# Two-level Strassen products in an MLP kernel: product 6 is also done in seven quarter products, and a pair's steps stand in another order

## The chip, the cores and the metric

The kernel runs on one core of one Trainium2 chip. The metric is device time in microseconds (us): the median of several executions of the whole kernel. The engines are named as in the profile: PE is the matmul engine (TensorE), PEld its weight loads, DVE is VectorE, ACT is ScalarE, POOL is GpSimd, SP is SyncE, which here issues transfers.

## The reference, cut to what matters

```python
batch, seq_len, hidden_dim = 8, 1024, 1024
intermediate_dim = 4 * hidden_dim

h = x @ w1                                   # [8192,1024] @ [1024,4096]
h = 0.5 * h * (1 + np.tanh(np.sqrt(2 / np.pi) * (h + 0.044715 * h ** 3)))
return (h @ w2).astype(np.float32)           # [8192,4096] @ [4096,1024]
```

Two large matrix products with a GELU between them. All of `x`, `w1`, `w2` arrive as float32 in device memory; the matmuls run on float16 copies and accumulate in float32.

## The kernel before, in words

**Blocks of tokens.** The 8192 tokens are worked in eight blocks of 1024 (`sb` 0 to 7). For each block a first stage computes `g = gelu(x @ w1)` and a second stage `g @ w2`. For blocks 0 and 1 the stages are `matmul1` and `matmul2_made`, which also build the operand sums and store them in device memory. For blocks 2 to 7, the late blocks, they are `matmul1_late` and `matmul2`, which load the stored sums. The change is about `matmul1_late`.

**Strassen, twice.** Every big product is cut in 2 by 2 blocks and done by the Winograd form of Strassen's method: seven products (numbered 1 to 7) of sums of blocks in place of eight. The dictionaries `W_SUM` and `S_SUM` name the sums: 5, 6, 7 and 4 on one side, 7, 6, 5 and 3 on the other. In the late blocks some of the seven products are cut once more in the same manner, into seven quarter products of half the size each way. In `matmul1_late` these are products 1, 5, 2 and 3; products 6, 7 and 4 are done whole. One whole product of a pair is two halves of four matmuls with 512 columns. One product of the second level is seven parts of two matmuls with 256 columns.

**Pairs.** `matmul1_late` goes through the 4096 intermediate columns in eight pairs (`Pair`, j = 0 to 7) of two chunks of 128 columns in each half of the intermediate dimension. A pair uses eight PSUM banks: a, b, c and d, each twice (h = 0, 1). In bank a, product 1 is followed by 6, 7 and 4; bank c holds 5, b holds 2, d holds 3.

**The order of the work is written out by hand.** The list `PAIR` is a string of keys, and `Pair.run` turns one key into instructions. `m` and `i` is a quarter product (`m15` is part 5 of product 1); `h60` is half 0 of the whole product 6; `c`, `a`, `p` and the keys `z11`, `z51` are ACT copies out of PSUM; the other `z`, the `e`, `s` and `u` are DVE additions; `g` is a GELU on ACT into the tile `g`; `d` is the subtraction `difference`. A key with a prime belongs to the previous pair, so that the end of one pair is woven into the next. After the last pair the list is walked once more for its primed keys alone: this is the tail of the stage. Every one of these instructions keeps its program order on its engine.

**What a product of the second level needs beside the matmuls.** For products 2 and 3 the base is a temporary (`a` or `s`); two DVE additions `e` add part 5 into it, and four DVE additions `z` write base plus running sum into the four quarters of the two banks, each between two parts. For products 1 and 5, whose base is zero, two of these steps are ACT copies.

**Operand sums.** The inner sums of the weights come from device memory (`s2`, `s3`; `s1` and `s5` for pairs 1 and 2) or are made on POOL from pair 3 on (`StoredHalf.make`, four operations a pair, one pair ahead). `StoredHalf` loads the weights of one pair in six groups (`GROUPS`) by SP's queue, two pairs ahead, into tiles of the pool `up` (26 tiles of 512 KB). The inner sums of x are made on DVE in tiles of the pool `gcp` (4 tiles): for product 2 in the stage before, for 1, 3 and 5 at the places that `X_SUMS` names, in pairs 0 and 1. Pair 0 does products 1 and 5 whole (`whole`), since the sums are not ready.

**Other work of the stage.** POOL also casts x of the next block through device memory (`x_cast_paced`, pairs 0 to 3; each starts behind a tiny copy that waits for a tile), does `difference`, and makes one sum for the second stage (`early.make(7, ...)`, after pair 5, into a `gcp` tile). In block 1, `matmul1` carries the `split_in_m1` jobs: the four inner sums of the second weight matrix for products 2 and 3, with loads and stores of their own.

## Time and profile before

| | us |
|---|---|
| median of 3 executions (1466.79 to 1467.35) | 1466.9 |
| the profiled execution's own time | 1466.68 |
| its span, first to last instruction | 1464.9 |
| PE busy in the span | 1456.8 (99%) |
| DVE busy | 1166.0 (80%) |
| ACT busy | 600.7 (41%) |
| POOL busy | 443.6 (30%) |
| one first stage of a late block (404.18 to 492.76) | 88.58 |
| one second stage of a late block (492.76 to 580.51) | 87.75 |

The page's own warning matters here: matmuls are pipelined and their ends are modelled, so a busy PE says nothing of how far apart the matmuls start. Durations are those of single instructions; where instructions follow each other closely, the distance between their starts is shorter than the duration, and it is the distance that counts in a queue. The granted clock of PE was 1.000 over the span.

### The profile page before, as it was taken

What the parts mean: (1) busy time and instruction counts of PE and PEld (TensorE: products, weight loads), DVE (VectorE), ACT (ScalarE), POOL (GpSimd) and SP (SyncE); (2) the same over time, 40 slices, a digit from 0 to 9 for tenths busy, and PEclk for the clock granted to TensorE, in tenths of its full rate; (3) what the DMA queues carried; (4) which work ended last, traced back from release to release, by engine and by line L of the source; (5) the groups of instructions that cost most, each with busy time, mean ns of one, the idle gap of its engine ahead of it and who ended that gap; (6) DMA issues with size and microseconds to landing.
All of it is one profiled execution on the core that took longest, in us unless ns stands there. A gap on an engine that the chain in (4) does not pass through costs nothing.

```text
span 1464.9 us, 27508 instructions
## 1 busy us (share of the span) xinstructions
PE 1456.8 (99%) x10383; PEld 1012.9 (69%) x10383; DVE 1166.0 (80%) x1940; ACT 600.7 (41%) x1226; POOL 443.6 (30%) x471
## 2 busy tenths in 40 slices
PE   8999999999999999999999999999999999999998
PEld 5444444444466788668876688767887678866787
DVE  6657459757677899879997799977998779887897
ACT  5665125631066411663126621366214652056410
POOL 1441123312347011560026501274103721136011
PEclk9999999999999999999999999999999999999999
DMA  9999899998998999979999899998999999996896
GB/s 330 342 349 392 229 342 360 385 300 230 353 323 215 360 276 366 375 207 373 307 369 338 203 373 326 359 305 248 350 346 347 297 280 313 352 367 215 310 302 206
DMA packets 207429, 462.15 MB, mean 315 GB/s; under 512 B 75840, under 2 KB 80960, under 8 KB 206400
## 3 DMA queue, kind: packets, MB, share of 16 engines
q1 hardware_dynamic: 179808, 364.96, 72.4%
q0 software_dynamic: 27488, 95.44, 21.9%
q8 instruction: 81, 1.33, 0.3%
q14 instruction: 52, 0.43, 0.1%
HBM read 361.76 MB, written 113.25 MB: 324 GB/s over the span
## 4 chain that ended last, share of the span: by engine, by line
PE 99%; DMA 1%; SPq 0%; DVE 0%; issue 0%; DVEq 0%
PE ps L1018 35%; PE ps L485 31%; PE ps L699 19%; PE ps L1059 13%; PE ps L418 1%; DMA gc<-in_w_dram 1%; SPq L159 0%; PE ps L395 0%; DVE u L223 0%; DVE u L135 0%; DVE u L406 0%; DVEq L135 0%
## 5 line engine op out<-in xcount | busy, mean ns | idle before, releaser
L485 PE MATMUL ps<-u 128*128 128x512 f16 x1808 | 423.5, 379 | 0.0
L135 DVE TENSOR_TENSOR tmp<-tmp,ps 128x512 f32<-128x512 f32 x498 | 280.3, 581 | 106.0 <-PE ps L485 44.6
L162 ACT COPY tmp<-ps 128x512 f32<-128x512 f32 (+1 forms) x398 | 209.4, 545 | 259.4 <-PE ps L1059 135.2
L135 DVE TENSOR_TENSOR ps<-tmp,ps 128x256 f32<-128x256 f32 x552 | 222.7, 425 | 102.9 <-PE ps L699 83.7
L1018 PE MATMUL ps<-u,gc 128*128 128x256 f16 x2688 | 300.3, 273 | 0.0
L485 PEld LDWEIGHTS <-u 128*128 128x128 f16 x1808 | 176.9, 98 | 170.2
L1018 PEld LDWEIGHTS <-gc 128*128 128x128 f16 x2688 | 263.0, 98 | 30.4
L699 PEld LDWEIGHTS <-u 128*128 128x128 f16 x2170 | 212.3, 98 | 67.9 <-issue 0.4
L498 ACT ACTIVATE g<-ps 128x512 f16<-128x512 f32 x326 | 192.9, 596 | 105.3 <-PE ps L699 64.9
L135 DVE TENSOR_TENSOR u<-u 128x2048 f16<-128x2048 f16 (+3 forms) x288 | 214.7, 787 | 23.6 <-DMA w_d<-u 10.9
L1018 PE MATMUL ps<-u,g 128*128 128x256 f16 x2016 | 227.9, 273 | 0.0
L162 ACT COPY u<-ps 128x512 f32<-128x512 f32 (+1 forms) x134 | 78.0, 587 | 354.9 <-PE ps L1018 348.0
L805 POOL DMA_DIRECT2D out_dram<-u x70 | 63.9, 936 | 498.2 <-DVE u L135 264.9
L1018 PEld LDWEIGHTS <-g 128*128 128x128 f16 x2016 | 197.2, 98 | 22.8
L699 PE MATMUL ps<-u 128*128 128x256 f16 x1298 | 193.6, 273 | 0.0
L135 DVE TENSOR_TENSOR u<-u,ps 128x512 f32<-128x512 f32 x216 | 147.7, 684 | 36.5 <-PE ps L1018 25.3
L1059 PE MATMUL ps<-u,g 128*128 128x512 f16 x768 | 166.4, 379 | 0.0
L498 ACT ACTIVATE g<-tmp 128x512 f16<-128x512 f32 x186 | 117.4, 633 | 99.0 <-DVE tmp L135 98.7
L306 POOL TENSOR_TENSOR u<-u 128x512 f16<-128x512 f16 x120 | 136.3, 1157 | 31.8 <-PE ps L699 22.4
L699 PE MATMUL ps<-gc,u 128*128 128x256 f16 x872 | 145.7, 273 | 0.0
L1059 PEld LDWEIGHTS <-g 128*128 128x128 f16 x768 | 75.1, 98 | 90.6
L1012 DVE TENSOR_TENSOR gc<-g,gc 128x2048 f16<-128x2048 f16 x84 | 102.4, 1220 | 3.1 <-PE ps L1018 3.1
(52 smaller groups left out, 854.8 us busy)
## 6 DMA issues: line engine op xcount, KB each, us to landing
u<-w_d SPq DMA_DIRECT2D x322, 512.0 KB, 9.1
u<-in_d SPq DMA_DIRECT2D x168, 512.0 KB, 7.9
out_dram<-u POOLq DMA_DIRECT2D x70, 512.0 KB, 10.8
gc<-in_w_dram SPq DMA_DIRECT2D x48, 512.0 KB, 6.0
g<-w_d SPq DMA_DIRECT2D x40, 512.0 KB, 12.0
w_d<-u POOLq DMA_DIRECT2D x36, 512.0 KB, 7.5
w_d<-u SPq DMA_DIRECT2D x32, 512.0 KB, 9.2
xb<-in_x_dram POOLq DMA_DIRECT2D x56, 256.0 KB, 6.8
```

The source lines that it names most:

```text
L135: i = nc.vector.tensor_tensor(out=out, in0=in0, in1=in1, op=op)
L162: tc.keep_in_program_order(nc.scalar.copy(out=out, in_=in_))
L306: nc.gpsimd.tensor_tensor(out=operand(j), in0=operand(u), in1=operand(v), op=op)
L418: tc.keep_in_program_order(nc.tensor.matmul(bank[:, cols], lhsT=w[:, k, :], rhs=self.xs.blocks[f"{a}{r}"][:, k, cols], start=r == 1 and k ...
L485: tc.keep_in_program_order(nc.tensor.matmul(bank, lhsT=w, rhs=x, start=first and k == 0, stop=k == n - 1, skip_group_check=not first,))
L498: gelu_last[0] = nc.scalar.activation(out=out, in_=src, func=GELU)
L699: tc.keep_in_program_order(nc.tensor.matmul(out, lhsT=w, rhs=x, start=first and k == 0, stop=k == 1, skip_group_check=not first,))
L805: return nc.gpsimd.dma_start(out=rows, in_=src, **kw)
L1012: tc.keep_in_program_order(engine.tensor_tensor(out=self.s[j], in0=in0, in1=in1, op=op))
L1018: tc.keep_in_program_order(nc.tensor.matmul(bank[:, i * OH // 2:(i + 1) * OH // 2], lhsT=t[:, c, i * P:(i + 1) * P], rhs=self.y[j][:, c, : ...
L1059: tc.keep_in_program_order(nc.tensor.matmul(pair(bank), lhsT=a[:, c, :], rhs=chunks(pieces[c // QC])[:, :, c % QC, :], start=(first and c ...
```

## The change

Product 6 joins the products of the second level in `matmul1_late`, from pair 1 on; pair 0 does 1, 5 and 6 whole. Its seven parts go into bank a, in which product 1 lay. The base of its additions is the ACT copy of product 1 (`temp a`), which was made before too, for product 2. Its first part starts the accumulation in bank a, h = 1, afresh. Two new DVE additions (`f60`, `f61`) write base plus part 5 into a new temporary `q`, because the copy itself is changed later by the additions `e` of product 2; four DVE additions `z61` to `z64` write the quarters. Added for this are the weight sums `s6`, which share a group with product 6 while 7 now shares one with 4, their making and storing in blocks 0 and 1 (`inner_sums(6)`), and four inner sums of x for product 6, in a fourth `gcp` tile. The sum that `early.make(7, ...)` makes goes to a tile of `up` instead.

The list `PAIR` is a new order. Products 2, 3, 6 (second half), 7 and 4 of a pair now run mostly within the next pair's walk. Pair 0 has a list of its own, `PAIR_FIRST`, and the sums of x stand there (four) and in pair 1 (the others). `difference` of pair 0 moves from DVE to POOL, and the first x cast of a stage waits for a sum of x instead of a GELU. `split_in_m1` is gone: its sums for products 2 and 3 are made in `matmul2_made` of block 0, as `split_jobs`, like that of product 1, in units of `up`.

```diff
-GROUPS = ((1, 5), ("s1", "s5"), (2, "s2"), (6, 7), (3, "s3"), (4,))
+GROUPS = ((1, 5), ("s1", "s5"), (2, "s2"), (6, "s6"), (3, "s3"), (7, 4))
...
+m15 m11 m51 e20' m26' z62' z53' z11 m55 m67' m63' c1 m54' p1' z22' z63' m27' z64' m23' c5 s0' m12
+m16 z12 z23' m22' m31' g110' m64' z24' s1' m35' h70' z31' m24' g111' m17 h71' z51 e31' z13 m36'
+u0' m14 a1 e30' m32' m56 h40' z32' m37' g210' z52 m13 m65 u1' m61 m53 z33' a0 m52 z34' f61 z61 m21
+m33' m25 h41' m62 f60 p0 m66 g221' g120' m57 g211' d' g220' e21 m34' z21 g121'
 """.split()
...
+PAIR_FIRST = """
+m11 i35 m21 m14 a0 i55 m25 a1 m51 p0 i65 e21 m61 i15 z21
 """.split()
-SPLIT_IN_M1 = (2, 3)
+X_SUMS = {
+    "g211'": ("i67",),
+    "c1": ("i66",),
+    "m56": ("i54",),
+    "z51": ("i14",),
+    "g121'": ("i64",),
+    "s0'": ("i17",),
+    "e20'": ("i16",),
+    "m23'": ("i57",),
+    "m37'": ("i34",),
+    "m26'": ("i36",),
+    "m67'": ("i56",),
+    "z22'": ("i37",),
+}
...
-            inner = ((2, 5, 3) if second else (1,)) if q == 0 else ((2, 3) if second else ())
+            inner = (2, 3) if second else (6,)
+            if q == 0:
+                inner += (5,) if second else (1,)
...
-            self.whole = (1, 5) if j == 0 else ()
+            self.whole = (1, 5, 6) if j == 0 else ()
...
-            b = {1: "a", 5: "c", 2: "b", 3: "d"}[m]
-            first = h == 1 and (b, 1) not in self.banks
+            b = {1: "a", 5: "c", 2: "b", 3: "d", 6: "a"}[m]
+            first = h == 1 and m not in self.begun
...
+            elif kind == "f":
+                add(temp("q", 0)[:, right if i else left], bank("a", 1)[:, right], temp("a", i)[:, right])
             elif kind in "ez":
-                b, t = ("b", "a") if m == 2 else ("d", "s")
+                b, t = {2: ("b", "a"), 3: ("d", "s"), 6: ("a", "a")}[m]
...
-                    add(bank(b, h)[:, cols], z, temp(t, h)[:, cols])
+                    base = temp(t, h)[:, cols]
+                    if m == 6 and cols == right:
+                        base = temp("q", 0)[:, right if h else left]
+                    add(bank(b, h)[:, cols], z, base)
...
-                spare = 0 < self.j < NI // 2 - 1
+                spare = self.j < NI // 2 - 1
...
-                    nxt["xb"] = x_cast_paced(sb + 1, g["11"][:, 2 * j, :], 2 * j, nxt.get("xb"), True)
+                    after = g["11"][:, 2 * j - 1, :] if j else xs.inner[5][:, 0, 0, :]
+                    nxt["xb"] = x_cast_paced(sb + 1, after, 2 * j, nxt.get("xb"), True)
...
-                early.make(7, nc.gpsimd)
+                early.make(7, nc.gpsimd, up, "u")
...
-        splits = {m: split_jobs(m, lambda m=m: pieces(m)) for m in (1, *SUMS)}
+        splits = {m: split_jobs(m, lambda m=m: pieces(m)) for m in (*W_TERM, *SUMS)}
```

More of the change, by code (lines that the diff above doesn't have):

```diff
@@ L28 @@
 PAIR = """
-m11 m36' m15 g111' z32' m21 h40' z11 c1 g221' m51 m37' g210' m55 z33' m25 c5 m12 z34' m16 z51
-h41' z12 m56 g211' m17 z52 m32' m13 z13 m33' a0 d' m52 m57 m53 g120' z21 m14 h60 p0 z53 e20 a1
-m54 s0 m34' p1 m26 m31 e21 m35 g121' h61 z22 z31 e30 m27 m22 s1 m23 h70 z23 g110 e31 z24 h71 u0
-m24 g220 u1
+m15 m11 m51 e20' m26' z62' z53' z11 m55 m67' m63' c1 m54' p1' z22' z63' m27' z64' m23' c5 s0' m12
+m16 z12 z23' m22' m31' g110' m64' z24' s1' m35' h70' z31' m24' g111' m17 h71' z51 e31' z13 m36'
+u0' m14 a1 e30' m32' m56 h40' z32' m37' g210' z52 m13 m65 u1' m61 m53 z33' a0 m52 z34' f61 z61 m21
+m33' m25 h41' m62 f60 p0 m66 g221' g120' m57 g211' d' g220' e21 m34' z21 g121'
 """.split()
-X_SUMS = """
-0z11:35 0z13:15 0z21:55 0z53:36 0a1:56 0m22:37 1m51:57 1m55:16 1m25:17 1z12:54 1m56:14 1h60:34
+PAIR_FIRST = """
+m11 i35 m21 m14 a0 i55 m25 a1 m51 p0 i65 e21 m61 i15 z21
 """.split()
-SPLIT_IN_M1 = (2, 3)
+X_SUMS = {
[12 more added lines that the diff above has]
+}
 def slots(table):
@@ L46 @@
     ;20:g50 w50 w51;21:g51 w52;22:w53 g52;23:g53 p14
-    ;50:w60 w61;51:w62 w63;52:g30 g31;53:g32 g33
-    ;60:w70 w71;61:w72 w73;62:w40 w41;63:w42 w43
-    ;73:x5;40:x7 x6;41:x3 q5;42:q6 q7 q4
-    ;43:i2 i3 i1 i5""".replace("\n    ", "")),
+    ;50:w60 w61;51:w62 w63;52:g30 g31 p25;53:g32 g33 p26
+    ;60:w70 w71 p27;61:w72 w73 p24;62:w40 w41;63:w42 w43
+    ;30:p35;31:p36;32:p37;33:p34
+    ;72:q5;73:q6 x5;40:q7 q4 x7;41:i2 i6 x6;42:i3 i1 x3
+    ;43:i5""".replace("\n    ", "")),
     slots("""10:g60 w50;11:g61 w51;12:g62 w52;13:g63 w53
@@ L539, in ahead @@
             jobs = [lambda m=m: quad.sum(m, pin=True) for m in ((7, 4) if second else (5, 6))]
-            inner = ((2, 5, 3) if second else (1,)) if q == 0 else ((2, 3) if second else ())
+            inner = (2, 3) if second else (6,)
+            if q == 0:
+                inner += (5,) if second else (1,)
             return jobs + [lambda m=m: quad.inner_sums(m) for m in inner]
         nxt = {}
-        splits = []
         late = None
@@ L603, in matmul1 @@
                 half = 3 if j % 2 else 0
-                if j != 4:
-                    jobs += splits
-                    splits = []
             for job in jobs[:half]:
@@ L648, in matmul1 @@
                 job()
-            if sb == 1 and j < 2 * len(SPLIT_IN_M1):
-                splits = split_in_m1(SPLIT_IN_M1[j // 2], j % 2)
             if sb == 1 and j > 4:
@@ L663, in __init__ @@
             self.j, self.source, self.xs, self.g = j, source, xs, g
-            self.whole = (1, 5) if j == 0 else ()
-            self.banks, self.temps = {}, {}
+            self.whole = (1, 5, 6) if j == 0 else ()
+            self.banks, self.temps, self.begun = {}, {}, set()
         def bank(self, b, h):
@@ L683, in part @@
             h, cols = {5: (1, right), 2: (0, left), 3: (0, right)}.get(i, (1, left))
-            b = {1: "a", 5: "c", 2: "b", 3: "d"}[m]
-            first = h == 1 and (b, 1) not in self.banks
+            b = {1: "a", 5: "c", 2: "b", 3: "d", 6: "a"}[m]
+            first = h == 1 and m not in self.begun
+            if first:
+                self.begun.add(m)
             out = self.bank(b, h)[:, cols]
@@ L708, in run @@
                 if i in (1, 4):
-                    self.half(m, int(i == 4), True)
+                    self.half(m, int(i == 4), m != 6)
             elif kind == "m":
@@ L713, in run @@
                 self.half(m, i, False)
-            elif kind in "cz" and m in self.whole:
+            elif kind in "czf" and m in self.whole:
                 pass
@@ L752, in matmul1_late, with x_sum @@
         made = set(xs.inner)
-        more = {
-            (int(k[0]), k[1:-3]): (int(k[-2]), int(k[-1])) for k in X_SUMS if int(k[-2]) not in made
-        }
+        def x_sum(key):
+            if int(key[1]) not in made:
+                xs.inner_sum(int(key[1]), int(key[2]))
         last = None
@@ L762, in matmul1_late @@
                 now = Pair(j, quads[j], xs, g)
-            for key in PAIR:
-                if key[-1] == "'":
-                    if last is not None:
-                        last.run(key[:-1])
+            for key in PAIR if j else PAIR_FIRST:
+                if key[0] == "i":
+                    x_sum(key)
+                elif key[-1] == "'":
+                    last.run(key[:-1])
                 elif j < n:
                     now.run(key)
-                    if (j, key) in more:
-                        xs.inner_sum(*more[j, key])
+                for job in X_SUMS.get(key, ()) if j == 1 else ():
+                    x_sum(job)
             last = now
@@ L948, in split_jobs @@
         return [lambda n=n: make(n) for n in SUMS]
-    def split_in_m1(m, h):
-        raw, t = [], {}
-        for k in range(2):
-            raw.append(gcp.tile([P, 2, HALF], DT, name="gc"))
-            q = 2 * k + h
-            nc.sync.dma_start(out=raw[k], in_=w2_at(q, m))
-        def make(i, n):
-            u, op, v = W_SUM[n]
-            if i % 2 == 0:
-                t["two"] = gcp.tile([P, 2, HALF], DT, name="gc")
-            t[n] = t["two"][:, i % 2]
-            in0, in1 = (
-                t[b] if isinstance(b, int) else raw[int(b[0]) - 1][:, int(b[1]) - 1] for b in (u, v)
-            )
-            tt(t[n], in0, in1, op, True)
-            nc.gpsimd.dma_start(
-                out=in_d[m][:, i, h * QC:(h + 1) * QC, :].rearrange("p c n -> p (c n)"), in_=t[n]
-            )
-        return [lambda i=i, n=n: make(i, n) for i, n in enumerate(SUMS)]
     def inner_block(t, b):
@@ L1006, in load_raw, with make @@
             )
-        def make(self, j, engine=nc.vector):
+        def make(self, j, engine=nc.vector, pool=gcp, name="gc"):
             u, op, v = S_SUM[j]
-            self.s[j] = gcp.tile([P, NI // 2, HT // 2], GT, name="gc")
+            self.s[j] = pool.tile([P, NI // 2, HT // 2], GT, name=name)
             in0, in1 = (self.s[t] if isinstance(t, int) else self.x[t] for t in (u, v))
```

## The prediction

> **What bounds the kernel now.** I read the page's busy times first, then what PE waited for, then the chain that ended last for the distance of matmuls, then the middle of a late first stage.

> ```profile
> PE 1456.8 (99%) x10383; PEld 1012.9 (69%) x10383; DVE 1166.0 (80%) x1940; ACT 600.7 (41%) x1226; POOL 443.6 (30%) x471
> ...
> L135 DVE TENSOR_TENSOR ps<-tmp,ps 128x256 f32<-128x256 f32 x552 | 222.7, 425 | 102.9 <-PE ps L699 83.7
> L306 POOL TENSOR_TENSOR u<-u 128x512 f16<-128x512 f16 x120 | 136.3, 1157 | 31.8 <-PE ps L699 22.4
> ...
> u<-w_d SPq DMA_DIRECT2D x322, 512.0 KB, 9.1
> ```
> ```profile
> PE ps L395 <- DVE tmp L387: 1.6, 4, 0.8
> PE ps L353 <- DVE warm L1153: 1.2, 1, 1.2
> PE ps L418 <- ACT u L162: 0.5, 1, 0.5
> PE ps L418 <- DVE u L223: 0.4, 1, 0.4
> ```
> ```profile
> 305.32 96.69 PE ps L1059 x448
> 492.76 85.59 PE ps L1018 x784
> ```
> ```profile
> 437.38:448.68 11.30, 11.30 (x83) 7.85 (x81) 8.47 (x20) 7.57 (x16) 7.87 (x9) 1.00 0.88 255
> 448.68:459.97 11.29, 11.29 (x82) 7.82 (x81) 8.48 (x20) 7.57 (x16) 7.37 (x6) 1.00 0.87 217
> 591.13:602.46 11.33, 11.33 (x82) 7.79 (x81) 9.60 (x24) 7.57 (x16) 2.00 (x4) 1.00 1.05 362
> ```
> ```profile
> 640.96 1.01 DVE L135 TENSOR_TENSOR tmp<-tmp,ps 128x256 f32<-128x256 f32 x2
> 641.89 0.42 DVE L135 TENSOR_TENSOR ps<-tmp,ps 128x256 f32<-128x256 f32 x1
> 642.22 0.41 DVE L135 TENSOR_TENSOR tmp<-tmp,ps 128x256 f32<-128x256 f32 x1
> 642.55 0.42 DVE L135 TENSOR_TENSOR ps<-tmp,ps 128x256 f32<-128x256 f32 x1
> ```

> The second fence lists every wait of PE: all lie in the start. From then on the kernel is one unbroken stream of matmuls, and only two things move its time: how long the stream is, and new waits. The third fence gives the stream's pace: a 512-column matmul every 96.69/448 = 0.2158 us, a 256-column one every 85.59/784 = 0.1092. The fourth (span, PE, PEld, DVE, ACT, POOL, clock, DMA share, GB/s) confirms it: a pair has four products of 14 small matmuls and three of 8 large ones, 56 x 0.1092 + 24 x 0.2158 = 11.29 us, the period seen. The fifth gives DVE's pace: 256-column additions start 0.33 us apart though each lasts 0.42, and a 512-column one (the second of the first row) takes 0.60 (641.29 to 641.89).

> **The change, part by part.**

> *Matmuls.* Per pair, 8 large ones (1.726 us) become 14 small ones (1.528): 0.198 us less. Pairs 1 to 7 of six blocks: 42 x 0.198 = 8.3 us off a stream with no slack. Firm.

> *DVE in a middle pair.* Before: 16 additions of 256 columns and 4 of 512, 16 x 0.331 + 4 x 0.598 = 7.7 us of queue. Six of 256 come on top: 9.7 of a period now 11.10. It fits, with 1.4 us to spare where 3.6 were. The new list leaves the second half of 2, all of 3, 7 and 4 to the next walk, so most additions have half a microsecond between the matmul that they read and the one that waits. What would wait first is `m12`, on the copy `z11`, which stands on ACT behind `g220'` and `g121'`; ACT has 16 operations and 7.57 us as before. A wait of PE holds its whole stream. I take 0 per middle pair; bounds 0 (PE has no such wait now) and 0.2 (half of an addition's duration).

> *Head of a stage (pairs 0 and 1).* Four sums more of x (0.33 us each on DVE) and PE arrives at the second level of product 1 earlier. In the block boundary seen,

> ```profile
> 578.18 1.03 PE L485 MATMUL ps<-u,g 128*128 128x512 f16 x4
> 579.06 1.22 DVE L135 TENSOR_TENSOR u<-u 128x2048 f16<-128x2048 f16 x1
> ```

> PE starts product 1 of the new block at 578.18 and DVE is free of the old stage's work at 579.06 + 1.13, 2.0 us later. From there, in order: the six DVE steps of `PAIR_FIRST` (2.0 us), `e20'` and the sums i16, i36, i56, i66 (1.7), then `z22'`, done at 2.0 + 2.0 + 1.7 + 0.4 = 6.1. `m27'` waits for it, and PE reaches that at 3.9 (four halves and two parts) + 1.1 (five parts) + 0.86 (`m54'`) = 5.85. Stall 0.3. Then 16 more small additions, 4 large and 8 sums, 10.4 us, up to `e20'` of pair 1, which `m26'` waits for: DVE 16.8, PE 16.5 plus the 0.3. Here DVE has no slack, and each pause of it is PE's: 0 to 0.6, I take 0.3. Head: 0.65, bounds 0.3 and 1.0, for five blocks; block 2 finds the sums of product 3 ready, so has four sums fewer and no loss.

> *Tail of a stage.* Before, the tail's matmuls were 5 parts and 2 halves (2.8 us) with three additions. Now 16 parts and 4 halves (6.95 us) alternate with 14 small and 4 large additions (7.0 us), and no other pair's matmuls lie between. With 0.2 us from a matmul's end to the addition (446.67 + 0.11 to 446.98 in the trace): `s0'` starts 1.5 us in, `s1'` 2.8, done 3.46; `h71'`, which waits for `s1'`, could start at 3.4; `u1'` is done at 6.14 and `h41'` could start at 6.1; m34' ends at 7.27. Loss 0.3 if DVE enters the tail with nothing pending; each 0.1 that it is late is paid by `h70'`, `h71'` and `h41'` in full. I take 0.55, bounds 0.2 and 0.9, six blocks.

> *Behind the tail.* `g220'` now comes last but one on ACT, and `difference` of pair 7 waits for `g211'`. The next stage's step 3 needs a sum made on DVE behind both: `difference` 0.7, then 1.22 for the sum; it is ready some 2.5 us after the tail, and steps 1 and 2 cover 32 x 0.109 = 3.5. Zero; without the cover 1 us a block at most. The second stage has DVE busy 81.3 of 87.75 us, so 0.4 us of lateness can be made good there.

> *POOL.* `d'` now waits for `g211'` late in the walk and blocks what is queued behind it: x's cast, `make` of the next pair. 2.13 + 4 x 1.16 + casts 1.2 = 8 of 11.1 us; the worst walk is that of pair 6, with `early.make` (4.1): `m15` needs the third of four sums, at 0.25 + 2.13 + 4.07 + 3.47 = 9.9 of 11.1. Zero, with 1.2 us of cover. `difference` of pair 0 on POOL takes 0.69 off DVE in the head, counted above.

> *Transfers.* 7 and 4 in one group and `s6`: 48 loads of 256 KB become 512 KB, 2.1 MB more a stage on 24 (273 GB/s x 88.6 us), and x's first cast starts earlier, when the share of DMA is already 1.05. Loads are issued two pairs (22 us) ahead, landing takes 9.1; tiles of `up` are held longer and `early.make` takes one more, so the lead shrinks, but 9 us are left. Zero; the upper bound is the late-data rival below.

> *Blocks 0 and 1.* Large matmuls with DVE near half busy in block 0; in block 1 sixteen splits of 0.69 us go, the inner sums for product 6 come. Both lie beside PE. Zero, ±0.5 us.

> Sum: -8.3 + 5 x 0.65 + 6 x 0.55 = -1.7 us. The profiled execution took 1466.7 (span 1464.9 and 1.8 around it): 1465.0. Its time stands 0.2 below the median of the runs shown: 1465.2.

> **The rivals.**

> *The ends hide it.* If DVE enters head and tail early, each costs its lower bound: 5 x 0.3 + 6 x 0.2 = 2.7, hence 1466.9 - 8.3 + 2.7 = 1461.3. For it: no wait of PE on DVE anywhere in the late stages now, and the old heads had eight to twelve sums too. Against: the counts above leave DVE 0.3 behind at `m27'` before any pause.

> *DVE becomes the bound in every pair (slower).* Deciding point: 0.2 us of wait per middle pair eats the whole gain, which is DVE's 26 operations costing 11.3 us in place of 9.7. If each held the engine for its full duration, 22 x 0.42 + 4 x 0.68 = 12.0, every pair would take 0.9 longer than PE's 11.1: 42 x 0.9 - 8.3 + the ends 6.6 = +36, 1503. At half that, 0.4 a pair, 1482; at 0.2 of waiting in each, 1473.6. Against it: the starts 0.33 apart in the fifth fence. [...] Read so, the 1503 would come true; this trace does not agree, since its operations start inside the duration of the one before, and of this rival's chance only 0.02 is for the full 0.9.

> *A weight or a POOL sum lands late (slower).* `m15` waits for POOL; if its walk of pair 6 runs 2 us late, 0.8 us x 6 and the same at DMA in pairs 1 to 3: 1465.2 + 5 to 8 = 1470 to 1473. DMA share 1.05 in pair 1 speaks for it, leads of over 9 us against.

> **How the numbers follow.** Change within 0.2% (2.9 us, about what a measurement of this kernel tells from none) has my forecast and most of its bounds. Losses at the ends under 5.4 us mean faster; the lower parts of their bounds and the first rival give that 0.33. The forecast's own case 0.48. The slower rivals: DVE 0.11, late data 0.08. So 0.33, 0.48, 0.19. Range: low 1460.3 (under the first rival), high 1471 (to the late-data case), leaving out the DVE rival and the smallest ends.

> **What would show it.** Part 1 of the page: 252 matmuls more, 252 DVE operations more for the pairs. Middle pairs 11.10 us long. PE's list of waits gets rows on DVE in the head and tail, a few tenths each; short ones may hide under the modelled ends, so the length of the stages is the better test: 88.6 before, about 88.4 after (88.58 - 1.39 + 1.2). I am wrong if middle pairs are longer than 11.2, if PE waits for POOL or DMA, or if the second stage is no longer 87.75.

## The result, and the profile after

The changed kernel takes 1490.96 us (median of 4 executions, 1488.94 to 1493.23) against 1466.95 before (4 executions, 1466.79 to 1467.35): ratio 1.0164, 95% interval 1.0146 to 1.0181, so 1.6% slower. The forecast was 1465.2, and the range up to 1471.0 does not hold the result. The profiled execution took 1490.02, with a span of 1488.2.

The first part of its page, and its list of what PE waited for (in all, times, longest; the rows of the start, which were there before, are left out):

```profile
PE 1460.1 (98%) x10635; PEld 1038.2 (70%) x10635; DVE 1263.1 (85%) x2226; ACT 612.2 (41%) x1226; POOL 457.1 (31%) x473
```
```profile
PE ps L711 <- DMA u<-w_d: 5.1, 4, 2.2
PE ps L711 <- POOL u L320: 4.3, 3, 2.6
PE ps L1057 <- DVE tmp L149: 3.8, 1, 3.8
PE ps L711 <- DVE tmp L149: 2.9, 4, 1.7
...
PE ps L499 <- DVE u L149: 1.8, 1, 1.8
```

The stream of matmuls, unbroken before, now waits for everybody: for weights (DMA), for sums made on POOL, for DVE in the late first stages (L711) and in blocks 0 and 1 (L1057, L499). Where that is, the lengths of the stages tell, from a stage's first matmul to the first of the next, in the profiled executions (the prediction counted 2.16 us of each first stage to the second: its 88.58 and 87.75 are 90.74 and 85.59 here):

| stage | before | after |
|---|---|---|
| block 0, second | 96.69 | 102.24 |
| block 1, first | 96.69 | 98.70 |
| block 2, first | 90.74 | 90.39 |
| blocks 3 to 7, first | 90.82, 91.05, 90.81, 90.81, 90.81 | 94.35, 95.32, 94.14, 93.48, 92.69 |
| blocks 2 to 7, second | 85.59 | 85.59 |

Block 0 and 1: +7.6 us. Late first stages: +15.3. Together 22.9 of the 23.3 by which the span grew; the rest is the start, whose length differs by about a microsecond between the profiled executions of these kernels (block 0's first run of 392 large matmuls begins at 27.2 us before, at 27.9 after, at 27.1 to 28.2 over all of them), and the end.

The middle pairs are not the place. Two of them in block 3 (span, PE, PEld, DVE, ACT, POOL, granted clock, DMA share, GB/s):

```profile
620.20:631.30 11.10, 11.10 (x89) 8.42 (x87) 10.34 (x27) 7.84 (x16) 7.75 (x9) 1.00 1.02 358
631.30:642.40 11.10, 11.10 (x89) 8.43 (x87) 10.34 (x27) 7.84 (x16) 7.75 (x7) 1.00 1.02 287
```

11.10 us, PE busy throughout: as forecast. All the loss beyond the forecast is in the first four pairs of a late block, and in blocks 0 and 1; the small waits of the tails are there too, and are taken up at the end.

One loss stands in none of the waits. After three of them (at 209.5, 605.5 and 796.6 us) the granted clock is 0.5 for 3.41 us. Two windows around the second, columns as above:

```profile
602.04:605.45 3.41, 1.55 (x13) 1.01 (x12) 3.41 (x5) 1.94 (x5) 2.97 (x4) 1.00 0.84 314
605.46:608.87 3.41, 3.41 (x18) 2.43 (x16) 2.19 (x6) 0.86 (x2) 0.41 (x1) 0.50 1.31 466
```

In the second window PE is never idle and yet runs at 0.50 of its clock; that costs about 1.7 us each time (half of 3.41), 5 in all.

### The profile page after: what moved, and what is told of

Read it like the earlier page. It is cut to its first block, busy times and chain, and to the rows that moved or that the text cites. A ratio compares the mean times of both kernels' runs of the same rounds, so it can differ in the third digit from the quotient of the medians.

```text
span 1488.2 us, 28427 instructions
## 1 busy us (share of the span) xinstructions
PE 1460.1 (98%) x10635; PEld 1038.2 (70%) x10635; DVE 1263.1 (85%) x2226; ACT 612.2 (41%) x1226; POOL 457.1 (31%) x473
## 4 chain that ended last, share of the span: by engine, by line
PE 81%; DVE 7%; DMA 7%; issue 2%; SPq 2%; POOL 1%; POOLq 0%; DVEq 0%
PE ps L1016 32%; PE ps L499 21%; PE ps L711 17%; PE ps L1057 10%; DMA u<-w_d 5%; DVE tmp L149 2%; DVE ps L149 2%; SPq L173 2%; DVE u L149 2%; DMA g<-w_d 2%; DVE gc L149 1%; PE ps L432 1%; POOL u L320 1%; DMA gc<-in_w_dram 1%; POOL xb L474 0%
## 5 line engine op out<-in xcount | busy, mean ns | idle before, releaser
L149 DVE TENSOR_TENSOR tmp<-tmp,ps 128x256 f32<-128x256 f32 (+1 forms) x582 | 312.9, 555 | 94.1 <-PE ps L499 38.6
L499 PE MATMUL ps<-u 128*128 128x512 f16 x1552 | 364.2, 379 | 2.7 <-DVE u L149 1.8
L149 DVE TENSOR_TENSOR ps<-tmp,ps 128x256 f32<-128x256 f32 x720 | 293.2, 425 | 34.2 <-PE ps L711 24.7
L711 PEld LDWEIGHTS <-u 128*128 128x128 f16 x2688 | 263.3, 98 | 80.8 <-DMA u<-w_d 6.2
L1016 PE MATMUL ps<-u,gc 128*128 128x256 f16 x2592 | 290.8, 273 | 0.0
L1016 PEld LDWEIGHTS <-gc 128*128 128x128 f16 x2592 | 253.6, 98 | 29.4
L149 DVE TENSOR_TENSOR u<-u 128x2048 f16<-128x2048 f16 (+3 forms) x320 | 231.9, 768 | 31.1 <-DMA u<-w_d 15.1
L499 PEld LDWEIGHTS <-u 128*128 128x128 f16 x1552 | 151.6, 98 | 151.0 <-issue 5.4
L711 PE MATMUL ps<-u 128*128 128x256 f16 x1520 | 229.6, 274 | 0.0
L711 PE MATMUL ps<-gc,u 128*128 128x256 f16 x1168 | 194.9, 274 | 9.4 <-DMA u<-w_d 5.1
L1057 PE MATMUL ps<-u,g 128*128 128x512 f16 x768 | 168.1, 381 | 3.8 <-DVE tmp L149 3.8
L518 POOL TENSOR_TENSOR g<-g,g 128x1024 f16<-128x1024 f16 x42 | 89.2, 2124 | 202.8 <-ACT g L512 202.8
L1057 PEld LDWEIGHTS <-g 128*128 128x128 f16 x768 | 75.5, 98 | 95.8 <-issue 6.3
## 6 DMA issues: line engine op xcount, KB each, us to landing
u<-w_d SPq DMA_DIRECT2D x365, 512.0 KB, 8.8
u<-in_d SPq DMA_DIRECT2D x168, 512.0 KB, 8.2
out_dram<-u POOLq DMA_DIRECT2D x70, 512.0 KB, 11.1
gc<-in_w_dram SPq DMA_DIRECT2D x48, 512.0 KB, 5.9
g<-w_d SPq DMA_DIRECT2D x45, 512.0 KB, 13.1
w_d<-u POOLq DMA_DIRECT2D x40, 512.0 KB, 6.1
w_d<-u SPq DMA_DIRECT2D x32, 512.0 KB, 8.9
in_d<-u POOLq DMA_DIRECT2D x28, 512.0 KB, 7.2
```

The costliest lines, as they stand in the source:

```text
L149: i = nc.vector.tensor_tensor(out=out, in0=in0, in1=in1, op=op)
L499: tc.keep_in_program_order(nc.tensor.matmul(bank, lhsT=w, rhs=x, start=first and k == 0, stop=k == n - 1, skip_group_check=not first,))
L518: tc.keep_in_program_order(engine.tensor_tensor(out=g["21"][:, cs], in0=g["11"][:, cs], in1=g["21"][:, cs], op=SUB,))
L711: tc.keep_in_program_order(nc.tensor.matmul(out, lhsT=w, rhs=x, start=first and k == 0, stop=k == 1, skip_group_check=not first,))
L1016: tc.keep_in_program_order(nc.tensor.matmul(bank[:, i * OH // 2:(i + 1) * OH // 2], lhsT=t[:, c, i * P:(i + 1) * P], rhs=self.y[j][:, c, : ...
L1057: tc.keep_in_program_order(nc.tensor.matmul(pair(bank), lhsT=a[:, c, :], rhs=chunks(pieces[c // QC])[:, :, c % QC, :], start=(first and c ...
```

## The experiments

All times are to be held against the kernel before, which ran beside each set: medians of 1466.7 to 1467.6 us. Two questions were followed: the heads of the late blocks, and blocks 0 and 1.

### First set: four single edits

My first theory had two parts. In block 0, DVE's queue stands still before a sum of weights that waits for a load. In the late blocks, weights come late because pair 0's walk has become short.

*Order of block 0's sums put back.* In these tables a step (product and number) stands left of the colon, and the jobs done there right of it: `q` is a sum of the first weights, `x` a sum of x, `i` inner sums, `w` a sum and `p` a split (an inner sum) of the second matrix.

```diff
-    ;72:q5;73:q6 x5;40:q7 q4 x7;41:i2 i6 x6;42:i3 i1 x3
-    ;43:i5""".replace("\n    ", "")),
+    ;73:x5;40:x7 x6;41:x3 q5;42:q6 q7 q4
+    ;43:i2 i6 i3 i1 i5""".replace("\n    ", "")),
```

> The kernel after, with one thing put back: in the second stage of block 0 the sums of the weight quad and of x stand in the order of before (x's sums ahead, sum 5 at step 1 of product 4 instead of after step 2 of product 7). Theory (a blocked queue): DVE stands 15.06 us before sum 5, which waits for a weight load, and everything of DVE behind it is late; then block 0's second stage falls from 102.24 to about 96.7 and block 1's first stage from 98.70 to about 96.7, 7.5 us off the profiled 1490.0, 1482.4; the drop of the granted clock at 209.5 us is gone. Rival (the inner sums of the second weight matrix, which moved from block 1 into block 0, load DVE or the queues too much): sum 5 is not the cause, block 0 stays within 1 us of 102.2, 1489 to 1491.

Measured: 1484.86 (1484.3 to 1486.46), ratio 1.0123 (1.0106 to 1.014), against the 1482.4 of the theory. Block 0's second stage is 96.69 again, and the half clock at 209.5 us is gone; block 1's first stays at 98.43. DVE's timeline at the end of block 0 (start, duration, operation, and in brackets the idle time before it and what ended it), first of the kernel after:

```profile
192.15 0.69 DVE L149 TENSOR_TENSOR tmp<-tmp,ps 128x512 f32<-128x512 f32 x1 [2.76 <-PE ps L1057]
207.90 1.23 DVE L149 TENSOR_TENSOR u<-u 128x2048 f16<-128x2048 f16 x1 [15.06 <-DMA u<-w_d]
209.04 0.68 DVE L149 TENSOR_TENSOR tmp<-tmp,ps 128x512 f32<-128x512 f32 x1
209.63 15.36 DVE L149 TENSOR_TENSOR u<-u 128x2048 f16<-128x2048 f16 x27
```

and of this experiment:

```profile
195.64 0.69 DVE L149 TENSOR_TENSOR tmp<-tmp,ps 128x512 f32<-128x512 f32 x1 [2.77 <-PE ps L1057]
196.24 5.00 DVE L149 TENSOR_TENSOR u<-u 128x2048 f16<-128x2048 f16 x4
207.86 2.48 DVE L149 TENSOR_TENSOR u<-u 128x2048 f16<-128x2048 f16 x2 [6.62 <-DMA u<-w_d]
```

In the kernel after, the sum at 207.90 holds up the addition of 209.04, which only needed PE's work of 195 us; product 4 waits for it, 3.8 us by the list above, and half clock follows. With the old order that addition runs at 195.64 and the sums of x use the idle time. The first half of the theory holds for block 0; for block 1 it doesn't.

*Another order of the loads.* Groups (1,5) and (s1,s5) of a pair go ahead of (3,s3) and (7,4) of the pair before, which are used some 12 us later.

```diff
+            if i > 1:
+                self.load(GROUPS[:2])
+                before.load(GROUPS[4:])
+                self.load(GROUPS[2:4])
+            else:
+                self.load(GROUPS if i == 0 else GROUPS[:4])
```

> The kernel after, with the same loads of the late blocks in another order on SP's queue: groups (1,5) and (s1,s5) of pair i now go ahead of (3,s3) and (7,4) of pair i-1, which are used about 12 us later. Theory (order and lead: pair 0's walk became 6.7 us shorter, so pair 2's first weights are wanted earlier, while the queue brings them behind weights of pair 1 that are wanted late): the waits of PE for DMA and for POOL in pairs 1 to 4 vanish, blocks 3 to 7's first stages come from 92.7 to 95.3 down to about 90.9, 13 to 16 us in all, 1474 to 1477. Rival (bytes: 2.1 MB more a stage are more than the DMA engines move in the time, whatever the order): the waits only change their place; 1488 to 1492.

Measured: 1488.57 (1487.19 to 1501.45), ratio 1.0164 (1.0122 to 1.0206). PE waits for DMA and POOL no more in the late blocks, as the theory had it, and nothing is gained: blocks 3 to 7 are 94.40, 92.68, 94.35, 92.68, 94.36. From block 2 on the main row of PE's waits is

```profile
PE ps L721 <- DVE tmp L149: 10.2, 5, 2.0
```

One wait on DVE in each block from 3 on, of the same size each time, ending 19.1 us into the stage. Something else had stood behind the late data, and the time is that of the rival (1488 to 1492), though not for the rival's reason: no data is late. This led to a sum of x and an operation of POOL, below.

*s6 left out.* This kernel leaves out the inner weight sums of product 6, so its output is not the reference's.

```diff
-GROUPS = ((1, 5), ("s1", "s5"), (2, "s2"), (6, "s6"), (3, "s3"), (7, 4))
+GROUPS = ((1, 5), ("s1", "s5"), (2, "s2"), (6, 7), (3, "s3"), (4,))
```

> The kernel after without the loads of s6 (256 KB less a pair; 7 goes with 6 again and 4 alone) and without the making and storing of s6; product 6's parts read product 6's own weights where s6 should stand, so the part of the output that product 6 feeds is not the reference's. All matmuls and additions stay. Theory bytes: without the 2.1 MB a stage that were added the waits of PE for DMA and POOL in the late blocks vanish, 13 to 16 us, 1474 to 1477. Theory order and lead: the second load of pair 2 comes at most some 1.3 us earlier than now, which is 17.6 us after the stage's start against 16.3 where PE wants it, so the waits shrink and don't vanish: blocks 3 to 7 stay 1 to 3 us above 90.9, 1478 to 1486. Both leave block 0's 102.2 within 1 us.

Measured: 1487.67 (2 executions). Neither number fits. Of the late data little is left in the late blocks (1.9 us for DMA in block 5, 1.1 for POOL in block 2), so the added bytes have a part in it as the order has; but the same wait on DVE stands in blocks 3, 4, 6 and 7, 2.0 us each. Block 0 took 105.12 and block 1's first stage 96.69.

*Pair 1 as late as before.*

```diff
+            if j == 1:
+                keep_clock(psum(), 30)
```

> The kernel after with 30 matmuls of 512 columns on a tile of zeros, 30 x 0.2158 = 6.5 us, between the short walk of pair 0 and pair 1 in each late block: pair 1 starts as late as it did before. Bytes and their order stay. Theory order and lead: the waits for DMA and POOL (15.7 us over five blocks, with the drops of the clock) vanish, and those for DVE at the stage's head (about 0.8 a block) too; 1490 + 6 x 6.5 - 15.7 - 3.9 = 1509. Rival bytes: the loads stay behind whatever the start, the waits come back some pairs later; 1490 + 39 = 1529, or down to 1520 if the head waits on DVE go.

Measured: 1511.03 (2 executions), for the 1509 of order and lead. All late waits in the heads but 0.2 us a block go, without a byte less. It is the early arrival of PE at pairs 1 to 3 that everything is late for. (Block 0 took 103.54 here.)

### A sum of x behind POOL

The kernel's tiles named here lie in SBUF, except `ps`, which lies in PSUM. "Port", in the expectations, is the name of a theory: POOL's operation holds up a DVE sum of two SBUF operands. The runs show the times; where in the chip the two meet, none shows.

DVE's and POOL's timelines of the kernel after at 602 us, in block 3:

```profile
602.24 0.42 DVE L149 TENSOR_TENSOR ps<-tmp,ps 128x256 f32<-128x256 f32 x1
602.58 2.29 DVE L149 TENSOR_TENSOR gc<-u,gc 128x512 f16<-128x512 f16 x1
604.79 0.41 DVE L149 TENSOR_TENSOR tmp<-tmp,ps 128x256 f32<-128x256 f32 x1
```
```profile
602.48 2.11 POOL L518 TENSOR_TENSOR g<-g,g 128x1024 f16<-128x1024 f16 x1 [12.10 <-ACT g L512]
```

The sum i64 (`gc<-u,gc`) takes 2.29 us where its likes take 0.42. It starts 0.1 us after POOL's `difference` of pair 0 and ends 0.28 us after it. That pair's difference is what the change moved from DVE to POOL. The same happens in blocks 5, 6 and 7 (2.29 to 2.30 us), and to no sum of this shape in the kernel before. In blocks 2 and 4 the same two meet, but there the sum starts 0.3 and 0.2 us ahead of POOL's operation, and it takes 0.42. DVE and then POOL in block 4:

```profile
782.51 0.42 DVE L149 TENSOR_TENSOR gc<-u,gc 128x512 f16<-128x512 f16 x1
```
```profile
782.71 2.20 POOL L518 TENSOR_TENSOR g<-g,g 128x1024 f16<-128x1024 f16 x1 [12.40 <-ACT g L512]
```

So in this profile the sum is long only where POOL has started first. The groups of this shape, before and then after (count, busy, mean ns):

```profile
L135 DVE TENSOR_TENSOR gc<-u,gc 128x512 f16<-128x512 f16 x34 | 13.7, 419 | 0.0
```
```profile
L149 DVE TENSOR_TENSOR gc<-u,gc 128x512 f16<-128x512 f16 x46 | 25.4, 582 | 0.0
```

46 x (582 - 419) = 7.5 us = 4 times 1.87. Two kernels tested that it is POOL's operation, and no wait for a tile or data. In the first, the sum stands twelve keys ahead in the list (the expectation says seven), and so ahead of `d'`, the difference:

```diff
-    "g121'": ("i64",),
+    "f60": ("i64",),
```

> The kernel after with one sum of x of the heads, i64, moved seven keys ahead, from g121' to f60, so that it no longer comes when POOL has just started the difference of pair 0. Nothing else. In the kernel after, and in the one with the other load order, this sum takes 2.30 us where its likes take 0.42, and ends 0.1 us after POOL's difference (2.11 us) ends; PE then waits 2.19 us in blocks 3, 5, 6 and 7. Theory port (a DVE sum of two SBUF operands stands still while POOL's operation reads SBUF): the sum takes 0.42, PE's waits on DVE at 17 to 19 us of a late stage go, and what is left in each stage is what the loads make late (1.4 in block 3, 3.1 in block 4, up to 2.4 and 1.3 in block 5, 0.8 in block 6); late stages 90.5 to 93.6, 1478 to 1485 in all. Rival (the 2.30 us is a wait for the sum's tile or its data): it takes as long in its new place or its successor does, 1488 to 1492.

Measured: 1487.96 (1485.88 to 1491.47), ratio 1.0146 (1.0132 to 1.0159). The theory's part on the sum is right. DVE and POOL in block 3:

```profile
601.19 0.42 DVE L149 TENSOR_TENSOR gc<-u,gc 128x512 f16<-128x512 f16 x1
...
602.52 0.42 DVE L149 TENSOR_TENSOR tmp<-tmp,ps 128x256 f32<-128x256 f32 x1
```
```profile
602.09 2.12 POOL L518 TENSOR_TENSOR g<-g,g 128x1024 f16<-128x1024 f16 x1 [12.10 <-ACT g L512]
```

0.42 us, the same operation on the same data. The addition of 602.52, which has one operand in PSUM, falls within POOL's 602.09 to 604.21 and takes 0.42 us too: POOL does not slow it. So the traces show the sum of two SBUF operands at 2.29 us behind POOL's difference, which reads SBUF, and at 0.42 ahead of it.

The time forecast for this run, 1478 to 1485, was missed; it is that of the rival (1488 to 1492), whose reason, a slow sum or successor, is refuted. What PE finds late now are weights: by the distances of its starts, block 3 has waits of 1.48 and 1.29 us, blocks 4 to 6 have 2.1 to 2.5 and 1.3 to 2.3. The chain that ended last, in block 3 of this run (start, duration, what it is):

```profile
594.03 18.10 DMA u<-w_d
612.35 1.16 POOL u L320
613.58 2.27 POOL u L320 x2
615.90 3.67 PE ps L711 x32
```

A load of half a megabyte lands 18.1 us after its issue, POOL makes its sums of it, PE waits for them.

In the second, the difference of pair 0 is on DVE, as before the change:

```diff
-                spare = self.j < NI // 2 - 1
+                spare = 0 < self.j < NI // 2 - 1
```

> The kernel after with the difference of pair 0 on DVE again, as before the change, and not on POOL. Theory port: no sum of x takes more than 0.5 us any more; DVE has 0.6 to 0.7 us more to do in pair 1, and waits for a GELU ahead of it, so PE waits for DVE about 0.7 to 1.2 in place of 2.19 a block, too short for the granted clock to drop; with the late loads left in, 1480 to 1487. Rival (DVE's load is what makes the 2.19): the waits grow by 0.6 a block, 1492 to 1495.

Measured: 1494.31 (1491.68 to 1499.4), ratio 1.0191 (1.0174 to 1.0207): no better than the kernel after. No sum is long any more, and DVE waits 0.36 us for the GELU in block 3. PE's waits in the late blocks are

```profile
PE ps L711 <- DMA u<-w_d: 9.9, 3, 4.8
PE ps L711 <- DVE tmp L149: 4.3, 4, 1.2
```

Those on DVE are 1.2 us at most, as the theory had it, and not the 2.8 of the rival, in whose range the time lies. The 1480 to 1487 was too good for another reason: in block 3 alone PE waits 4.7 us for weights. With POOL free, the second cast of x starts at 598.1 in place of 604.9 us, and the load that PE needs lands 24.3 us after its issue, against 22.6 in the run with the sum moved. That the cast is what delays the load was not tried alone.

So the two causes hide each other. Blocks 3 to 7, first stages, the sum over 5 x 90.80:

| | loads as after | loads in the other order |
|---|---|---|
| sum i64 behind POOL | 16.0 (after) | 14.5 |
| sum i64 ahead | 14.1 | 0.2 (next run) |

(The next run has two repairs of blocks 0 and 1 besides.) Either repair alone gains 1.5 to 2 us; both together 15.8.

### The repairs together, and a filled tail

Four repairs: the order of block 0's sums, the order of the loads, i64 at f60, and the four inner sums for product 6 of the first quad (a quad is the weights of two pairs) in block 1's second pair:

```diff
+            if sb == 1 and j == 1:
+                jobs.append(lambda: quads[0].inner_sums(6))
```

> The kernel after with four repairs together: the order of block 0's sums as in the first experiment, the four inner sums for product 6 of the first weight quad moved out of block 0's last steps into block 1's second pair, the other load order, and the sum i64 ahead of POOL's difference. Theory (a blocked DVE queue in block 0, DVE work piled up ahead of block 1, the port in the heads, late loads): all waits go but those of the heads and tails (0.45 and 0.67 a block); block 0's second and block 1's first stage 96.7 each, late first stages 90.5; 1490.0 - 5.55 - 2.0 - 17.5 = 1465.0, give or take 1.5. Rival (bytes, or a further wait behind those): any of these stages stays more than 1 us longer; over 1468.

Measured: 1470.63 (11 executions, 1466.49 to 1473.87), ratio 1.0018 (1.0008 to 1.0027). The late first stages are 90.05, 90.98 and four times 90.80, near the 90.5 expected. Block 0's second and block 1's first are 99.12 and 98.66 in the profiled execution, not 96.7, and the time is the rival's (over 1468): with the old order of the sums back, PE itself waits 2.3 us for the raw weights of block 1.

With the tails filled by matmuls that are ready early:

```diff
+BEGIN = {"h70'": 1, "h71'": 3, "h41'": 3}
...
+                    if j == n and sb < NSB - 1:
+                        early.begin(BEGIN.get(key, 0))
```

> The kernel with the four repairs, and in the tails of blocks 2 to 6 seven of the sixteen matmuls of the first step of the second stage's product 4 (they need GELUs of pairs 0 to 3 alone, and weights that are loaded a pair ahead) stand between the tail's own: one ahead of h70', three ahead of h71', three ahead of h41'. Theory (the tail's 0.67 us is PE waiting for a chain of DVE additions): the tail's waits vanish in five blocks, 3.3 us less than the kernel with the repairs, 1461.7. Rival (the chain's end is only moved: the third step of product 4 then waits for its sum of GELUs, which DVE makes after the tail): the second stages get a wait of about as much, 1464 to 1466.

Measured: 1465.28 (11 executions, 1463.53 to 1468.86), ratio 0.9992 (0.9983 to 1.0001); the profiled execution took 1464.3. Of the tail's 0.67 us all but 0.13 is gone in five blocks: first stages (seven matmuls longer) and second stages are 91.03 and 84.82 together, 175.85, against 90.80 and 85.59, 176.39; 0.54 us a block. The second stage got no wait, so the rival is refuted, but the 1461.7 was missed too. This is the best of all, and not told apart from the kernel before. All that PE waits for in it behind the start, by its list of waits:

```profile
PE ps L724 <- DVE tmp L150: 0.8, 5, 0.2
```

The list hides what falls under the modelled ends of matmuls; by the distances of their starts the heads still lose 0.77 us in each of five blocks.

In this execution blocks 0 and 1 are at 96.69 and 96.81, with the same program there as in the kernel with the repairs. What these two stages cost changes between executions; why it changes was not found.

### Blocks 0 and 1: work with no room

Windows at 164 to 188 us, before and after (columns as above; the last but one is the DMA share):

```profile
164.00:176.00 12.00, 12.00 (x57) 5.45 (x56) 9.41 (x9) 0.95 (x2) 1.07 (x2) 1.00 0.55 123
176.00:188.00 12.00, 12.00 (x58) 5.43 (x56) 2.12 (x4) 0.00 (x0) 1.69 (x4) 1.00 0.83 205
```
```profile
164.00:176.00 12.00, 12.00 (x58) 5.41 (x56) 9.37 (x11) 1.17 (x2) 1.06 (x2) 1.00 1.26 278
176.00:188.00 12.00, 12.00 (x57) 5.46 (x56) 10.11 (x16) 0.00 (x0) 4.85 (x9) 1.00 0.97 274
```

The splits that the change moved into block 0 fill a stretch in which the DMA engines had been partly free (shares of 0.55 and 0.83). SP's queue there, before and after:

```profile
166.22 21.67 SPq L159 DMA_TRANSPOSE u<-xb  x16
187.93 3.78 SPq L159 DMA_DIRECT2D w_d<-u  x4
```
```profile
164.94 26.60 SPq L173 DMA_TRANSPOSE u<-xb  x16
191.58 3.51 SPq L173 DMA_DIRECT2D w_d<-u  x4
```

The transposes of x take 4.9 us longer, and the raw weights of block 1's first quad, from which DVE makes the sums, stand behind them. The sum that waits for them starts at 207.90 (202.07 before). Eight kernels moved the splits about. The first three put them back into block 1 with the code of before (`split_in_m1`, pairs 0 to 3): in the kernel with the repairs, in that with the filled tails too, and in the kernel after alone.

```diff
-    ;60:w70 w71 p27;61:w72 w73 p24;62:w40 w41;63:w42 w43
-    ;30:p35;31:p36;32:p37;33:p34
+    ;60:w70 w71;61:w72 w73;62:w40 w41;63:w42 w43
...
+            if sb == 1 and j < 2 * len(SPLIT_IN_M1):
+                splits = split_in_m1(SPLIT_IN_M1[j // 2], j % 2)
```

> The kernel with the four repairs, and the splits of the second matrix for products 2 and 3 back in block 1, as they were before the change, and out of block 0's second stage. In the kernel with the repairs the raw weights of the first quad land at 210 to 214 us in one profile and at 204 to 210 in that of the kernel with the filled tail, against 202 to 207 before the change, and the time of the runs is spread over 7 us. Theory (the splits in block 0, their stores and the loads behind them, make these loads late, by an amount that changes from run to run): block 0's second and block 1's first stage are 96.7 in every run, the runs lie within 3 us of each other, 1465.0 (1464.3 to 1466). Rival (the splits have no part in it; the sums or x's transposes are late of themselves): the spread stays, 1468 to 1472.

> The same with the tails filled too. Theory: 0.6 us in each of five blocks less than the one without, 1462.0, below the kernel before by 4 to 5 us with a narrow spread. Rival (spread and level of the kernel with the filled tail, 1463.5 to 1468.9, come from elsewhere): 1464 to 1466 with the same spread.

> The kernel after with the splits alone moved back to block 1; the order of block 0's sums stays the new one, and so do the late blocks. Theory (two causes that add up: loads that land late, and a DVE queue that stands before them): the loads land some 2 to 4 us earlier, so block 0's second stage is 98 to 101 in place of 102.2, and block 1's first stage at most 98; 1484 to 1488. Rival (the order alone decides): block 0 stays at 102, 1489 to 1492. Rival (the splits alone decide): both stages 96.7, 1482.

Measured: 1472.11 (1470.43 to 1475.99), 1471.16 (1468.8 to 1475.16) and 1488.18 (1486.67 to 1489.63); ratios 1.0036 (1.0024 to 1.0049), 1.0028 (1.0016 to 1.004) and 1.0145 (1.0129 to 1.016). Block 0 is at 96.69 in all three, in the third even with the new order of the sums, which starts its first weight sum at 201.17 there: the late loads and the order are both needed for that wait of DVE. (Late loads alone can make PE wait at the start of block 1, as in the kernel with the repairs.) But block 1's first stage grows to 100.4, 102.6 and 100.0; it has new work of its own: the inner sums of product 6 (DVE sums `u<-u` of 128x512: 76 in the kernel before, 92 after, most of the new ones in block 1) and their stores. That these are the cause was not tried alone. The first two missed their theories by 6 to 9 us, and their runs spread over 5.6 and 6.4 us. The second also had 3.9 us of waits for POOL in blocks 4 and 5, the longest 2.5, so the repaired heads have little margin.

The rest looked for room. The splits for product 3 went to block 1's pairs 6 and 7; with those for product 2 in pairs 4 and 5 too; or to the ends of pairs 4 and 6 alone (one line of each of the three kernels):

```diff
+SPLIT_IN_M1 = {5: ((3, 0),), 6: ((3, 1),)}
...
+SPLIT_IN_M1 = {3: ((2, 0),), 4: ((2, 1),), 5: ((3, 0),), 6: ((3, 1),)}
...
+SPLIT_IN_M1 = {3: ((3, 0),), 5: ((3, 1),)}
```

> The kernel with the four repairs and the filled tails, with the splits for product 3 of the second matrix moved out of block 0 (178 to 185 us) into pairs 6 and 7 of block 1; those for product 2 stay in block 0. Theory (DVE work and the loads behind it pile up at 165 to 256 us): block 0's second and block 1's first stage come to 96.7 each, the runs scatter by less than 3 us, 1462 to 1464. Rival (the added inner sums for product 6 and their stores are the cause): as the kernel with the filled tails, 1464 to 1469 with its scatter.

> The same, with the splits for product 2 moved too, into pairs 4 and 5 of block 1, so that block 0 has none. Theory: as the one before or better, since block 0 then has the work it had before the change; both stages 96.7, 1462 to 1463.5. Rival (pairs 4 and 5 have no room beside the sums of the fourth quad): block 1's first stage over 97.5, 1464 to 1468.

> The kernel with the four repairs and the filled tails, with the splits for product 3 moved out of block 0 to the ends of pairs 4 and 6 of block 1; those for product 2 stay in block 0. Theory (the added work fits where neither DVE's sums nor the loads of the next stage stand): all of block 0's and block 1's stages 96.7, scatter under 3 us, 1461.5 to 1463.5, below the kernel before by 3 to 5. Rival (no room: the transfers of block 1's second half are needed for the next stage): block 1's second stage over 97.5, as with pairs 6 and 7, 1465 to 1474.

And four splits went ahead of a sum for which DVE waits, in block 0 itself, in the kernel after alone and in the best kernel:

```diff
-    ;60:w70 w71 p27;61:w72 w73 p24;62:w40 w41;63:w42 w43
-    ;30:p35;31:p36;32:p37;33:p34
+    ;60:p27 p24 w70 w71;61:p35 p36 w72 w73;62:w40 w41;63:w42 w43
+    ;30:p37;31:p34
```

> The kernel after with four of block 0's splits (p27, p24, p35, p36) ahead of the sums w70 and w72 that wait for stores, in DVE's idle time at 155 to 164 us. Nothing else. Theory (the splits' stores at 164 to 188 crowd the transposes of x and so the raw weights): the raw weights land 2 to 5 us earlier, at 203 to 206, block 0's second stage is 97 to 100 in place of 102.2; 1483 to 1488. Rival (bytes: the stores only crowd what goes at 155 to 170, w70's store comes later and so does all behind it): 102 or more, 1489 to 1493.

> The kernel with the four repairs and the filled tails, with the same four splits put ahead. Theory: block 0's second and block 1's first stage 96.7 in every run, 1462 to 1464, scatter under 3 us. Rival: as without it, 1464 to 1469 or more.

| splits of products 2, 3 | time, us | ratio, interval | block 0 second | block 1 first | block 1 second | block 2 first |
|---|---|---|---|---|---|---|
| 3 in pairs 6, 7 | 1474.30 | 1.0055 (1.0042 to 1.0067) | 96.69 | 100.24 | 104.36 | 90.28 |
| both late | 1487.69 | 1.0150 (1.0128 to 1.0173) | 96.69 | 106.64 | 103.99 | 96.18 |
| 3 in pairs 4, 6 | 1469.49 | 1.0022 (1.0005 to 1.0038) | 96.69 | 97.82 | 96.69 | 94.88 |
| early, kernel after | 1489.58 | 1.0153 (1.0139 to 1.0167) | 100.76 | 98.93 | 96.69 | 90.08 |
| early, best kernel | 1466.49 | 0.9998 (0.9989 to 1.0007) | 98.21 | 98.69 | 96.69 | 90.27 |

All five missed their theory's number. Where product 3's splits leave block 0, its end is clean; then the waits come in block 1, or in block 2's head. In the six runs without them in block 0 the transposes take 21.4 to 22.2 us; moved ahead within block 0 they leave the transposes at 26.6 us (30.6 in the best kernel). So it is not when DVE makes them, as I had thought, but that they are made and stored there at all; which of the two it is was not tried alone. Long transposes are not enough for a wait: in the profiled execution of the best kernel they took 26.45 us and block 0 was at 96.69. That DVE's busy times of 12 to 18 us in 24 mean room was wrong too. No place was found that costs nothing; whether there is one stays open.

## Why the prediction was wrong

*Matmuls, -8.3, and DVE in a middle pair, 0:* right. Middle pairs are 11.10 us, without a wait.

*Head, 0.65, and tail, 0.55 a block:* right in place, somewhat small. (The head's two stalls of 0.3 make 0.6, not 0.65.) In the kernel with the repairs, where nothing else hides them, the head's waits, by the distances of PE's starts, are 0.15, 0.30 and 0.32 (0.77), of which the prediction had the last two, and the tail's 0.08, 0.31 and 0.28 (0.67). With 7 x 0.198 = 1.39 gained a block, this leaves 0.05 lost: measured 90.80 against 90.81, so the same within 0.1. The change is worth its matmuls and pays them all back at the ends.

*Behind the tail, 0:* right, second stages are 85.59 as before.

*"`difference` of pair 0 on POOL takes 0.69 off DVE":* here the prediction failed first. It counted what leaves DVE and not what POOL then does to DVE: 1.87 us on one sum in four blocks; in blocks 2 and 4 the sum came first by 0.2 to 0.3 us, which is luck. Where no late load hides it, in the run with the other load order, that is 2.2 us of PE's time in each of five blocks.

*"Transfers ... landing takes 9.1 ... 9 us are left. Zero":* wrong. 9.1 is the median of the whole kernel; in the heads, where the profile showed a share of 1.05, loads land 15 to 24 us after their issue. They did so before the change too, and the trace of before could have told it. Here are the loads of weights issued around the start of block 3 with the least, median and greatest time to landing in us, before and then after:

```profile
L281 SPq DMA_DIRECT2D u<-w_d x10: 319/320/320, 569.2 to 589.8; - x10
DMA to landing us min/median/max: 13.6/18.4/21.1
```
```profile
L295 SPq DMA_DIRECT2D u<-w_d x11: 319/319/320, 576.2 to 599.4; - x11
DMA to landing us min/median/max: 15.6/18.2/22.6
```

So the loads hardly became slower; PE came earlier. The lead was counted in pairs of 11 us, though the new pair 0 lasts 3.9. The rival "a weight or a POOL sum lands late" had the right mechanism, 0.8 us a wait and a chance of 0.08; the waits were up to 2.6 us.

*"Blocks 0 and 1 ... Zero, ±0.5":* wrong by 7.6 us. "Both lie beside PE" was true of DVE's busy time and not of its order: a sum moved ahead of an addition brings its own wait with it, 5.55 us in block 0, which the first experiment took back. That splits moved into block 0 take transfers with them was not looked at.

These two steps, POOL's difference and the lead, make the 16.0 us that the first stages of blocks 3 to 7 stand above 90.80; neither alone explains them, since each hides the other.

*Not in the prediction at all:* the half clock after a wait, 5 us in the profiled execution (1.7 of it within the 7.6 of blocks 0 and 1).

The rival "DVE becomes the bound in every pair", which had most of the slower side's chance, is refuted: 10.34 us of DVE in 11.10, no wait.

## What to carry to other kernels

Work moved to another engine must be costed against what runs on the old one at that moment: here a POOL operation of 2.1 us that reads SBUF stretched a DVE sum of two SBUF operands from 0.42 to 2.29 us wherever POOL had started first, by as little as 0.1 us. When one stage is shortened, recount every lead that was measured in it, from the landing times in that stage and not from the kernel's median; and when a repair gains nothing, look for the second wait that ends at the same place before dropping it.

## What the hardware showed beyond expectation

The clock. In the run with the other load order five equal waits of 2.2 us were followed by half clock in blocks 3, 5 and 7 and by none in 4 and 6 (94.4 against 92.68 us: 1.7). Windows of that run, in block 3 and in block 4 (columns as above):

```profile
602.34:605.75 3.41, 1.38 (x13) 1.09 (x12) 3.41 (x6) 1.19 (x4) 3.08 (x4) 1.00 0.90 333
605.76:609.16 3.40, 3.40 (x18) 2.44 (x17) 2.44 (x6) 1.46 (x3) 0.99 (x1) 0.50 1.09 375
783.26:786.66 3.40, 1.86 (x18) 1.66 (x18) 3.37 (x8) 0.86 (x4) 2.15 (x4) 1.00 0.98 394
786.68:790.08 3.40, 3.40 (x26) 2.29 (x24) 3.37 (x9) 1.82 (x4) 2.11 (x2) 1.00 1.21 361
```

The 26 matmuls behind the wait show it in all five blocks, 3 to 7: by the chain that ended last they take 4.67, 3.00, 4.67, 3.00 and 4.51 us.
